# Joining two weight groups at the start, moving constant loads, and forming norm factors in columns

## The chip, the cores and the metric

The kernel runs on one core of one Trainium2 chip. The metric is device time in microseconds (us) of the whole kernel; lower is better. The engines are PE (TensorE, matrix products), DVE (VectorE), ACT (ScalarE), POOL (GpSimd) and SP (SyncE, which here only issues DMAs). Each engine works through its own instructions strictly in the order in which they stand.

## The reference, cut to what matters

Two transformer blocks of width 2048 run one behind the other on 256 tokens, all in float32. Every projection is preceded by a root-mean-square norm:

```python
def rmsnorm(x, g):
    x32 = x.astype(jnp.float32)
    y = x32 * lax.rsqrt(jnp.mean(x32 * x32, axis=-1, keepdims=True) + EPS)
    return (y * g.astype(jnp.float32)).astype(x.dtype)
...
    hn = rmsnorm(h, norm_mix_g)
    proj = hn @ w_in + b_in          # q, k, v, gates, conv inputs
    ... mLSTM, conv, merge: h = h + merged @ w_out
    hn = rmsnorm(h, norm_ffn_g)      # up, depthwise conv, silu, down
    ...
    return rmsnorm(h, norm_out_g)    # and the second block starts:
h = rms_norm(x, g_pre); y = gla_mixer(h, ...); x = x + rms_norm(y, g_post)
h = rms_norm(x, g_pre); y = mla_mixer(h, ...); x = x + rms_norm(y, g_post)
# in mla_mixer: c_q, c_kv, k_rope, gate = split(h @ w_in)
#   q = rms_norm(c_q, g_qa) @ w_qb ; kv = rms_norm(c_kv, g_kva) @ w_kvb
```

The norm factor is one number for each token. The kernel multiplies by it after the projection, so a projection need not wait for it, but its results do.

## The kernel before, in words

All weights are read once, as one stream of pieces of about 1 MB that SP issues in a fixed order into three buffers (`raw`). A piece has two halves of up to 1040 columns, called subs here. For each sub ACT writes the rounded high part and DVE the remainder into a tile `hl` (lines 312 and 313); there are four such tiles, and the split is asked for three subs ahead of use (`LOOK`). Activations are held with features on the 128 partitions and tokens along the row, split in the same way (`xhl`, lines 434 and 435).

PE multiplies group by group. A group of kind A has blocks of 128 output features; each unit (a block of weights for one k of 16) is a pair of matmuls, 512 and 256 columns (lines 359 and 360). A group of kind B (`v`, `gv`) has tokens on the partitions and 344 features along the row, three matmuls for each k and each half of the tokens (lines 372 to 374). Results stand in two double accumulators in PSUM (`acc`) and are taken out by `evac`: ACT copies one half to `t`, DVE adds the other (`u`, lines 412 and 413).

At the start the x tiles `h`, the first weight pieces and then the constants (`con`, with the identity and a matrix of ones; `vec`, with gains and biases) come through SP. The first groups are four `qk` groups (a head's q and k blocks each), then three `v` groups. POOL meanwhile works through some 55 instructions that make the angle tables for the rotary embedding (`rope_tables`), and behind those, in its own order, issues the three DMAs of the `v` bias (`vb`, line 731). The results of the first `v` group (`ifc`, line 735) need `vb`; three matmuls into the second `v` group, PE transposes `ifc` (line 654).

A norm factor is formed in two shapes. `bc_sum` multiplies a matrix of ones by the squares, which puts the sum of every token on all partitions, a row of 256 numbers; ACT takes the root and DVE the reciprocal of 128x256 (`rsqrt`, lines 465 and 466). `col_sum` gives the same sums as two columns of 128 tokens, one token on a partition. The places that matter are `mk_R1` (row `R` and column `Rc` of the first norm, within the fourth `qk` group), `mk_R3` (behind the second block's first q and k groups: output norm of block one and the next norm combined, rows `Ro` and `R`, column `Rc`), the last input norm (`st6`, in the first `mgate` group) and `low_rank_scale` (factors `sq` and `skv`, after the second `mgate` group). In `mk_R3`, `Rc` is needed by `gkc` (line 892), which PE transposes three matmuls into the second `gv` group (line 902). POOL multiplies `h` by `Ro` (`x2_scale`, line 1001).

Instructions come in program order except for a priority: what stands in `tc.high_priority(offset=150)` is ordered as if written 150 places earlier. `tc.issue_after(st["mm"])` puts a small matmul behind the last group's.

Of the kernel before, what the change touches and what calls it, by code (L numbers as in the profile page):

```python
# [8 lines left out]
F32 = mybir.dt.float32  # L9
F32R = mybir.dt.float32r  # L10
I32 = mybir.dt.int32
AF = mybir.ActivationFunctionType
ALU = mybir.AluOpType

P = 128
T = 256
D = 2048
KD = D // P
# [11 lines left out]
VB = 344  # L30
# [4 lines left out]
def _blk(start, n=P):  # L35
    return np.arange(start, start + n)
# [9 lines left out]
def plan():  # L46
# [14 lines left out]
        g.append(dict(name=name, kind=kind, blocks=blocks, k0=k0, nk=nk, n=nk * n, order=order))  # L61

    W = "w_in"
    for h in range(4):
        add("qk", "A", [(W, _blk(h * P)), (W, _blk(512 + h * P))], 0, KD)
    vcols = np.concatenate([_blk(3072, 8), _blk(1024, 1024)])
    for c in range(3):
# [175 lines left out]
def build(tc, a, dump=None):  # L243
# [26 lines left out]
    def vc(name, i):  # L270
        return vec[:, vw[name] + i:vw[name] + i + 1]
# [4 lines left out]
    def tt(name="t"):  # L276
        return tp.tile([P, 2, T], F32, tag="t2", name=name)

    def sm(name="sm"):
        return smp.tile([P, 512], F32, tag="sm", name=name)  # L280
# [15 lines left out]
    def piece_dma(p, x, y_):  # L296
        at, n = pieces[p]
        src = stream[P * at:P * (at + n)].rearrange("(p n) -> p n", p=P)
        nc.sync.dma_start(raws[p][:, x:y_], src[:, x:y_])

    def need(q_):
        while st["sub"] <= min(q_, len(subs) - 1):
            q = st["sub"]
            p, half = divmod(q, 2)
            emit_dma(p + RAW - 1)
            n = subs[q]
            o = subs[q - 1] if half else 0
            hl = hlp.tile([P, 2, SUB], F32R, tag="hl", name="hl")
            cuts = (0, n) if q else (0, n // 2, n)
            for x, y_ in zip(cuts, cuts[1:]):  # L310
                src = raws[p][:, o + x:o + y_]
                S.activation(hl[:, 0, x:y_], src, AF.Copy)  # L312
                V.tensor_tensor(hl[:, 1, x:y_], src, hl[:, 0, x:y_].bitcast(F32), op=ALU.subtract)  # L313
            hls[q] = hl
            if half == 1:
                raws.pop(p, None)
            hls.pop(q - 8, None)
            st["sub"] += 1
# [87 lines left out]
    def bc2(r):  # L406
        return r[:, None, :].to_broadcast([P, 2, T])

    def evac(ps, nb=2):
        t, u = tt("t"), tt("u")  # L410
        with tc.high_priority(offset=150):
            S.activation(halves(t[:, :nb]), out_of(ps[:, :nb, T:2 * T]), AF.Copy)  # L412
            V.tensor_tensor(halves(u[:, :nb]), out_of(ps[:, :nb, 0:T]), halves(t[:, :nb]), op=ALU.add)  # L413
        return u
# [10 lines left out]
    def split(dst, src, scale=None):  # L425

        v = dst.rearrange("p (a s i) -> p s a i", a=2, s=2)
        hi, lo = v[:, 0], v[:, 1]
        src = halves(src)
        if scale is None:  # L430
            i = S.activation(hi, src, AF.Copy)
            j = V.tensor_tensor(lo, src, hi.bitcast(F32), op=ALU.subtract)
        else:
            i = S.activation(hi, src, AF.Identity, scale=scale)
            j = V.scalar_tensor_tensor(lo, src, scale, hi.bitcast(F32), op0=ALU.mult, op1=ALU.subtract)  # L435
        return i.ins, j.ins
# [26 lines left out]
    def rsqrt(out, in_, scale):  # L463

        S.activation(out, in_, AF.Sqrt, bias=epsc[:out.shape[0]], scale=scale)
        V.reciprocal(out, out)

    def bc_sum(ss):
        ps = sm()
        with tc.issue_after(st["mm"]):  # L470
            PE.matmul(ps[:, 0:T], lhsT=ones, rhs=ss, start=True, stop=True)
        return ps[:, 0:T]

    def col_sum(ss):
        ps = sm()
        for t in range(2):
            with tc.issue_after(st["mm"]):
                PE.matmul(ps[:, t:t + 1], lhsT=ss[:, t * P:(t + 1) * P], rhs=ones[:, 0:1], start=True, stop=True)
        return ps[:, 0:2]

    def out_norm(name, IN, g, y):

# [37 lines left out]
    def lazy(X_, f, ahead):  # L520

        done = [0]

        def get(k):
            while done[0] <= min(k + ahead, KD - 1):
                f(done[0])
                done[0] += 1
            return X_(k)

        return get  # L530
# [17 lines left out]
    xload = lambda x, y_: nc.sync.dma_start(h[:, x:y_], a["xT"][:, x:y_])  # L548
    s0, n0, n1 = subs[0], pieces[0][1], pieces[1][1]
    xload(0, 1)  # L550
    piece_dma(0, 0, s0 // 2)
    xload(1, 2)
    xload(2, 4)
    piece_dma(0, s0 // 2, s0)
    xload(4, 6)
    piece_dma(0, s0, n0)
    xload(6, 8)
    xload(8, 10)
    piece_dma(1, 0, subs[2])
    xload(10, 12)  # L560
    xload(12, 14)
    piece_dma(1, subs[2], n1)
    xload(14, 16)
    emit_dma(2)
    nc.sync.dma_start(con, a["con"])
    nc.sync.dma_start(vec[:, 16:nvec], a["vec"][:, 16:nvec])
    _, X = hl_tiles(2, "xhl")
    need(0)
    for k in range(KD):
        split(X(k), h[:, k], vc("g_mix", k))  # L570
        if k in (2, 6, 10):
            need(k // 4 + 1)
    st1 = Stat("a")

    R = row_tile("R")
# [1 line left out]

    def mk_R1():
        ss = st1.fold(V)
        rsqrt(R, bc_sum(ss), 1.0 / D)  # L580
        rsqrt(Rc, col_sum(ss), 1.0 / D)

    COS, SIN = row_tile("COS"), row_tile("SIN")
    turn = inv_two_pi()
# [46 lines left out]
    def qk_out(hd, u):  # L631
        uR = times_R(u, R)
        S.activation(qk[:, hd, 0], uR[:, 0], AF.Identity, bias=vc("bq", hd))
        V.tensor_scalar(qk[:, hd, 1], uR[:, 1], vc("bk", hd), float(P) ** -0.5, op0=ALU.add, op1=ALU.mult)

    held = []
    for hd in range(4):
        u = evac(dense("qk", X))
        held.append(u)
        for k in ((0, 2, 4), (6, 8, 10), (12, 14), ())[hd]:  # L640
            st1.add(h[:, k:k + 2], eng=V)
        if hd == 2:
            mk_R1()
        if hd >= 2:
            while held:
                qk_out(hd + 1 - len(held), held.pop(0))
    ccol = stp.tile([P, 2, 4], F32, tag="ccol", name="ccol")
    rw = lambda i: rows[0:4, i, :]

# [78 lines left out]

    for c in range(3):
        vb = tt("vb").rearrange("p a t -> p (a t)")  # L730
        nc.gpsimd.dma_start(vb[:, 0:VB], a["bv"][c:c + 1, :].to_broadcast([P, VB]))
        ps = dense("v", X)
        ifc = tt("ifc")
        for t in range(2):
            stt = lambda dst, x, y_: V.scalar_tensor_tensor(dst, ps[:, t, x:y_], Rc[:, t:t + 1], vb[:, x:y_],
                                                            op0=ALU.mult, op1=ALU.add)
            if c == 0:
                stt(ifc[:, t, 0:8], 0, 8)
                stt(vm[:, t, 0:VB - 8], 8, VB)
            else:  # L740
                stt(vm[:, t, c * VB - 8:(c + 1) * VB - 8], 0, VB)
        if c == 0:
            side.append(mlstm_rows(ifc))
        pump()
# [120 lines left out]

    def mk_R3():
        s3, s4 = st3.fold(), st4.fold()
        for (ro, r, f) in ((Ro, R, bc_sum), (None, Rc, col_sum)):
            n = T if f is bc_sum else 2
            w = tt("w")  # L870
            ro = ro if ro is not None else w[:, 1, 0:n]
            rsqrt(ro, f(s3), 1.0 / D)
            t = w[:, 0, 0:n]
            V.tensor_tensor(t, f(s4), ro, op=ALU.mult)
            V.tensor_tensor(t, t, ro, op=ALU.mult)
            rsqrt(t, t, 1.0 / D)
            V.tensor_tensor(r, t, ro, op=ALU.mult)

    gb = big(name="gb")
    gbT = gb[:, 0:2048].rearrange("p (b t) -> p b t", b=8)  # L880
# [185 lines left out]
    gates = big(F32, (P, KD, T), name="gates")  # L1066

    def low_rank_in(which, s, q, ps):
        u = evac(ps)
        s.add(u)  # L1070
        for b in range(2):
            i = 2 * q + b
            split(cqkv[:, 4 * which + i], u[:, b], vc(("g_qa", "g_kva")[which], i))

    def low_rank_scale(s, tag):
        ss = s.fold()
        r = row_tile(tag)
        w = tt("w")
        V.tensor_tensor(w[:, 0], R, R, op=ALU.mult)
        V.tensor_tensor(w[:, 1], bc_sum(ss), w[:, 0], op=ALU.mult)  # L1080
        rsqrt(w[:, 1], w[:, 1], 1.0 / 512)
        V.tensor_tensor(r, w[:, 1], R, op=ALU.mult)
        return r

    sa, sb = Stat("a"), Stat(None, gates[:, 14:16])
    ps = dense("cq", X)
# [20 lines left out]
    for j in range(8):  # L1107
        u = evac(dense("mgate", X))
        if j == 0:
            rsqrt(R, bc_sum(st6.fold()), 1.0 / D)  # L1110
            uR = times_R(ukr, R, 1)
            rope([(kr[0:64, 0], 0, 64), (kr[64:128, 1], 64, 128)], uR[:, 0], (V, V, G, G))
        s = times_R(u, R, eng=G)
        S.activation(gates[:, 2 * j:2 * j + 2], s, AF.Silu)
        if j == 1:
            sq_ = low_rank_scale(sa, "sq")
            skv = low_rank_scale(sb, "skv")
        if j == 2:
            pc = sm()
            for t in range(2):  # L1120
                PE.transpose(pc[:, t:t + 1], skv[0:1, t * P:(t + 1) * P], con[0:1, C_ID:C_ID + 1])
            skc = stp.tile([P, 2], F32, tag="Rc", name="skc")
            V.tensor_copy(skc, pc[:, 0:2])

    _, OX = hl_tiles(2, "ohl")
    XQ = lambda k: cqkv[:, k]
# [125 lines left out]
```

## Time and profile before

| | before |
|---|---|
| runs | 2059.97, 2060.18, 2061.51 us; median 2060.18 us |
| profiled execution | 2059.47 us, span 2057.8 us (1.67 us lie around it) |
| PE busy | 2005.0 us, 97% of the span |
| DVE, ACT, POOL busy | 70%, 56%, 19% |
| mean granted clock of TensorE | 0.990 |
| HBM read | 381.52 MB, 186 GB/s over the span |

A PE that is busy 97% of the time sets the time; what can be won is in its idle time, some 53 us, and in stretches in which its clock is granted at half. An engine's idle time elsewhere costs nothing by itself.

### The profile page before, as it was taken

To read this page: it belongs to the slowest core of one execution; us is meant where nothing else is said; L and a number is where in the kernel's file an instruction comes from. 1 tells how busy PE (TensorE), PEld (TensorE's weight loads), DVE (VectorE), ACT (ScalarE), POOL (GpSimd) and SP (SyncE) were. 2 spreads that over 40 slices of the span, in tenths; PEclk is the share of its full clock that TensorE was granted. 3 is DMA by queue.
4 is the path that set the end of the run, shared out by engine and by line. 5 is a ranking of instruction groups with operands and counts; after the bars stand their busy time and mean duration, and the time that the engine had idled before them with its cause. 6 is when DMAs were issued, how large, how long until landed. Compare 5 with 4: busy or idle time off the path is not lost. (4 is left out here: it accounts for less than half of the span.)

```text
span 2057.8 us, 30674 instructions
## 1 busy us (share of the span) xinstructions
PE 2005.0 (97%) x12438; PEld 1849.7 (90%) x12438; DVE 1433.7 (70%) x1758; ACT 1153.3 (56%) x1599; POOL 392.9 (19%) x333
## 2 busy tenths in 40 slices
PE   8799999999999999999999999999999999999997
PEld 7788999999999999999999999989999988989996
DVE  7568776666667888864588876676767558777754
ACT  6454555555556666654466666655666556544453
POOL 8511000010122111100011113321220025112312
PEclk9999999999999999999999999999999999999998
DMA  7443555555555555555555555535545544554343
GB/s 289 155 164 144 204 200 204 191 204 204 205 201 188 205 204 198 198 200 206 203 205 203 197 195 206 205 120 198 180 171 188 201 170 178 194 188 145 109 165 112
DMA packets 55743, 385.61 MB, mean 187 GB/s; under 512 B 6384, under 2 KB 6640, under 8 KB 10544
## 3 DMA queue, kind: packets, MB, share of 16 engines
q1 hardware_dynamic: 55152, 382.91, 51.5%
q8 instruction: 97, 1.59, 0.3%
q0 software_dynamic: 304, 0.73, 0.1%
q14 instruction: 46, 0.38, 0.1%
q10 hardware_dynamic: 144, 0.01, 0.0%
HBM read 381.52 MB, written 2.10 MB: 186 GB/s over the span
## 5 line engine op out<-in xcount | busy, mean ns | idle before, releaser
L313 DVE TENSOR_TENSOR hl<-raw,hl 128x1024 fp32r<-128x1024 f32 (+3 forms) x722 | 941.0, 1311 | 353.3 <-ACT hl L312 352.8
L359 PE MATMUL acc<-xhl,hl 128*128 128x512 f32 x3440 | 1138.1, 384 | 9.5 <-DVE xhl L435 7.8
L312 ACT ACTIVATE hl<-raw 128x1024 fp32r<-128x1024 f32 (+3 forms) x722 | 756.8, 1052 | 395.3 <-PE acc L360 250.5
L360 PE MATMUL acc<-xhl,hl 128*128 128x256 f32 x3440 | 940.9, 274 | 1.6 <-DVE hl L313 1.6
L359 PEld LDWEIGHTS acc<-xhl,hl 128*128 128x128 f32 x3440 | 652.6, 190 | 105.0 <-DVE xhl L435 6.9
L360 PEld LDWEIGHTS acc<-xhl,hl 128*128 128x128 f32 x3440 | 662.7, 193 | 3.3 <-DVE hl L313 2.9
L359 PE MATMUL acc<-ghl,hl 128*128 128x512 f32 x688 | 225.4, 382 | 0.0
L412 ACT ACTIVATE t<-acc 128x512 f32<-128x512 f32 x138 | 82.2, 596 | 192.6 <-PE acc L360 171.8
L360 PE MATMUL acc<-ghl,hl 128*128 128x256 f32 x688 | 187.5, 273 | 0.0
L413 DVE TENSOR_TENSOR u<-acc,t 128x512 f32<-128x512 f32 x138 | 94.9, 688 | 104.3 <-ACT t L412 104.3
L418 POOL TENSOR_TENSOR uR<-u,R 128x512 f32<-128x512 f32 x51 | 69.8, 1369 | 443.3 <-DVE u L413 436.0
L359 PEld LDWEIGHTS acc<-ghl,hl 128*128 128x128 f32 x688 | 130.0, 189 | 18.1
L360 PEld LDWEIGHTS acc<-ghl,hl 128*128 128x128 f32 x688 | 132.1, 192 | 0.0
L456 POOL TENSOR_TENSOR ss<-ss,sq 128x512 f32<-128x512 f32 x41 | 64.9, 1584 | 223.0 <-ACT sq L451 213.6
L374 PE MATMUL acc<-hl,xhl 128*128 128x344 f32 x288 | 90.4, 314 | 1.5 <-DVE hl L313 1.5
L372 PE MATMUL acc<-hl,xhl 128*128 128x344 f32 x288 | 91.0, 316 | 0.0
L373 PE MATMUL acc<-hl,xhl 128*128 128x344 f32 x288 | 90.3, 313 | 0.0
L795 POOL TENSOR_TENSOR m<-u 128x256 f32<-128x256 f32 x16 | 24.9, 1553 | 336.1 <-DVE u L793 336.1
L783 PE MATMUL acc<-hmxc,hl 128*128 128x512 f32 x256 | 84.7, 382 | 0.0
L359 PE MATMUL acc<-mg,hl 128*128 128x512 f32 x256 | 83.9, 382 | 0.0
L831 ACT ACTIVATE cv<-uR,vec 128x256 f32<-128x256 f32 x86 | 46.9, 593 | 57.9 <-POOL uR L418 57.9
L359 PE MATMUL acc<-ohl,hl 128*128 128x512 f32 x224 | 73.7, 383 | 0.0
(515 smaller groups left out, 2490.2 us busy)
## 6 DMA issues: line engine op xcount, KB each, us to landing
raw<-stream SPq DMA_DIRECT2D x330, 1024.0 KB, 4.8
raw<-stream SPq DMA_DIRECT2D x21, 1032.0 KB, 4.8
raw<-stream SPq DMA_DIRECT2D x4, 512.0 KB, 7.2
out<-y SPq DMA_DIRECT2D x8, 256.0 KB, 2.1
h<-xT SPq DMA_DIRECT2D x7, 256.0 KB, 7.2
raw<-stream SPq DMA_DIRECT2D x1, 1028.0 KB, 4.7
raw<-stream SPq DMA_DIRECT2D x1, 1008.0 KB, 4.7
raw<-stream SPq DMA_DIRECT2D x1, 988.0 KB, 6.6
```

What stands on the lines that cost most here:

```text
L312: S.activation(hl[:, 0, x:y_], src, AF.Copy)
L313: V.tensor_tensor(hl[:, 1, x:y_], src, hl[:, 0, x:y_].bitcast(F32), op=ALU.subtract)
L359: PE.matmul(o, lhsT=wh, rhs=both(x), start=(k == 0), stop=False)
L360: mm = PE.matmul(o[:, T:2 * T], lhsT=wl, rhs=part(x, 0), start=False, stop=(k == nk - 1))
L372: PE.matmul(o, lhsT=xh, rhs=both(wh), start=(k == 0), stop=False)
L373: PE.matmul(o, lhsT=xl, rhs=both(wh), start=False, stop=False)
L374: mm = PE.matmul(o, lhsT=xh, rhs=both(wl), start=False, stop=(k == nk - 1))
L412: S.activation(halves(t[:, :nb]), out_of(ps[:, :nb, T:2 * T]), AF.Copy)
L413: V.tensor_tensor(halves(u[:, :nb]), out_of(ps[:, :nb, 0:T]), halves(t[:, :nb]), op=ALU.add)
L418: (eng or V).tensor_tensor(w[:, :nb], u[:, :nb], bc2(R)[:, :nb], op=ALU.mult)
L456: (eng or G).tensor_tensor(self.ss, self.ss, sq, op=ALU.add)
L783: PE.matmul(o, lhsT=wh, rhs=both(x), start=(k == 0), stop=False)
```

## The change

The first two `qk` groups become one group of four blocks, which runs over the first eight k for all four blocks, then over the last eight for two blocks at a time. The x tiles are split as the group asks for them (`lazy`), not all ahead; the first weights come in smaller cuts, later x tiles in larger ones. The two evictions of the joined group, and one pair in the last layer, are taken out of the early order (`ahead=0`). `con` and the rest of `vec` are loaded behind this group. The squares of `h` are added during the third and fourth `qk` groups, and `mk_R1` with all four `qk_out` follows the fourth. `vb` is loaded through SP. At `mk_R1`, `mk_R3`, the last input norm and `low_rank_scale` only the two columns are formed (`second` combines two norms in a column), and `to_row` spreads a column along the row: DVE multiplies the identity by the column (`dg`), PE multiplies ones by `dg`, ACT copies the result.

```diff
-    for h in range(4):
+    add("qk", "A", [(W, _blk(o + h * P)) for h in range(2) for o in (0, 512)], 0, KD)
+    for h in (2, 3):
         add("qk", "A", [(W, _blk(h * P)), (W, _blk(512 + h * P))], 0, KD)
...
-            cuts = (0, n) if q else (0, n // 2, n)
+            cuts = (0, n) if q else (0, n // 4, n // 2, n)
...
-    def evac(ps, nb=2):
+    def evac(ps, nb=2, ahead=150):
         t, u = tt("t"), tt("u")
-        with tc.high_priority(offset=150):
+        with tc.high_priority(offset=ahead):
...
+    def to_row(dst, c_):
+
+        dg, pr = tt("dg"), sm()
+        for t in range(2):
+            V.tensor_scalar(dg[:, 0, t * P:(t + 1) * P], ident, c_[:, t:t + 1], None, op0=ALU.mult)
+            with tc.issue_after(st["mm"]):
+                PE.matmul(pr[:, t * P:(t + 1) * P], lhsT=ones, rhs=dg[:, 0, t * P:(t + 1) * P], start=True, stop=True)
+        S.activation(dst, pr[:, 0:T], AF.Copy)
...
+    def second(dst, c_, total, n):
+
+        w = col_tile("cw")
+        V.tensor_tensor(w, total, c_, op=ALU.mult)
+        V.tensor_tensor(w, w, c_, op=ALU.mult)
+        rsqrt(w, w, 1.0 / n)
+        V.tensor_tensor(dst, w, c_, op=ALU.mult)
...
-    nc.sync.dma_start(con, a["con"])
-    nc.sync.dma_start(vec[:, 16:nvec], a["vec"][:, 16:nvec])
+    xload(12, 16)
     _, X = hl_tiles(2, "xhl")
-    need(0)
-    for k in range(KD):
-        split(X(k), h[:, k], vc("g_mix", k))
-        if k in (2, 6, 10):
-            need(k // 4 + 1)
+    X_ = X
+    X = lazy(X_, lambda k: split(X_(k), h[:, k], vc("g_mix", k)), 4)
...
         ss = st1.fold(V)
-        rsqrt(R, bc_sum(ss), 1.0 / D)
         rsqrt(Rc, col_sum(ss), 1.0 / D)
+        to_row(R, Rc)
...
     held = []
+    ps = dense("qk", X)
+    nc.sync.dma_start(con, a["con"])
+    nc.sync.dma_start(vec[:, 16:nvec], a["vec"][:, 16:nvec])
+    held += [evac(p_, ahead=0) for p_ in ps]
+    X = X_
+    for hd in (2, 3):
+        for k in range(8 * hd - 16, 8 * hd - 8, 2):
+            st1.add(h[:, k:k + 2], eng=V)
+        held.append(evac(dense("qk", X)))
+    mk_R1()
     for hd in range(4):
-        u = evac(dense("qk", X))
-        held.append(u)
...
+        qk_out(hd, held[hd])
...
-        nc.gpsimd.dma_start(vb[:, 0:VB], a["bv"][c:c + 1, :].to_broadcast([P, VB]))
+        nc.sync.dma_start(vb[:, 0:VB], a["bv"][c:c + 1, :].to_broadcast([P, VB]))
...
         s3, s4 = st3.fold(), st4.fold()
-        for (ro, r, f) in ((Ro, R, bc_sum), (None, Rc, col_sum)):
...
+        t3, t4 = col_sum(s3), col_sum(s4)
+        c3 = col_tile("c3")
+        rsqrt(c3, t3, 1.0 / D)
+        second(Rc, c3, t4, D)
+        to_row(R, Rc)
+        to_row(Ro, c3)
...
-    def low_rank_scale(s, tag):
-        ss = s.fold()
+    def low_rank_scale(s, tag, c6):
+        c_ = col_tile("c" + tag)
+        second(c_, c6, col_sum(s.fold()), 512)
         r = row_tile(tag)
...
+        to_row(r, c_)
+        return r, c_
...
-            rsqrt(R, bc_sum(st6.fold()), 1.0 / D)
+            c6 = col_tile("c6")
+            rsqrt(c6, col_sum(st6.fold()), 1.0 / D)
+            to_row(R, c6)
...
-            sq_ = low_rank_scale(sa, "sq")
-            skv = low_rank_scale(sb, "skv")
-        if j == 2:
-            pc = sm()
-            for t in range(2):
-                PE.transpose(pc[:, t:t + 1], skv[0:1, t * P:(t + 1) * P], con[0:1, C_ID:C_ID + 1])
-            skc = stp.tile([P, 2], F32, tag="Rc", name="skc")
-            V.tensor_copy(skc, pc[:, 0:2])
+            sq_, _ = low_rank_scale(sa, "sq", c6)
+            skv, skc = low_rank_scale(sb, "skv", c6)
```

Lines of the changed kernel lie up to 17 higher than those of the kernel before. SP's queue at the start, before (`raw` are weight pieces, `h` x tiles; pieces of 2064 columns belong to the `v` groups):

```order
L299 DMA raw<-stream 128x2048
L565 DMA con<-con 128x1408
L566 DMA vec<-vec 128x564
L299 DMA raw<-stream 128x2048 x5
L299 DMA raw<-stream 128x2064 x8
```

The same queue now:

```order
L569 DMA h<-xT 128x1024
L300 DMA raw<-stream 128x2048 x5
L653 DMA con<-con 128x1408
L654 DMA vec<-vec 128x564
L300 DMA raw<-stream 128x2064 x5
L748 DMA vb<-bv 128x344
L300 DMA raw<-stream 128x2064 x2
L748 DMA vb<-bv 128x344 x2
```

The constants moved behind five more weight pieces, and `vb` now stands on SP, the first behind the fifth `v` piece; the fifth to eighth `v` pieces are used by the second and third `v` groups.

DVE at `mk_R3`, before, from the eviction of the k group (`w` are scratch, `q_` and `uR` use the row `R`, `gkc` and `vg` use the column `Rc`):

```order
L413 TENSOR_TENSOR u<-acc,t 128x512
L466 RECIPROCAL R<-R 128x256
L313 TENSOR_TENSOR hl<-raw,hl 128x1032
L874 TENSOR_TENSOR w<-sm,R 128x256
L466 RECIPROCAL w<-w 128x2
...
L466 RECIPROCAL w<-w 128x256
L466 RECIPROCAL w<-w 128x2
L313 TENSOR_TENSOR hl<-raw,hl 128x1032
L877 TENSOR_TENSOR R_11748<-w,R 128x256
L877 TENSOR_TENSOR Rc<-w 128x2
L1007 SCALAR_TENSOR_TENSOR q__11952<-u,R_11748 128x512
```

DVE at the same place now (`c_11936` is the column `c3`):

```order
L467 RECIPROCAL c_11936<-c_11936 128x2
L497 TENSOR_TENSOR cw<-sm,c_11936 128x2
L498 TENSOR_TENSOR cw<-cw,c_11936 128x2
L314 TENSOR_TENSOR hl<-raw,hl 128x1032
L467 RECIPROCAL cw<-cw 128x2
L314 TENSOR_TENSOR hl<-raw,hl 128x1032
L500 TENSOR_TENSOR Rc<-cw,c_11936 128x2
L486 TENSOR_SCALAR dg<-con,Rc 128x128 x2
L486 TENSOR_SCALAR dg<-con,c_11936 128x128 x2
L314 TENSOR_TENSOR hl<-raw,hl 128x1032
L1020 SCALAR_TENSOR_TENSOR q__11959<-u,R_11752 128x512
```

The operations on 128x256 are gone, `Rc` stands behind two weight splits (`hl`), not four, and four `dg` are new. On PE the four matmuls that read `dg` stand 39 matmuls into the first `gv` group.

ACT at `low_rank_scale`, before, from the eviction of the second `mgate` group (`gates` is a silu of another table):

```order
L412 ACTIVATE t<-acc 128x512
L312 ACTIVATE hl<-raw 128x1024
L1114 ACTIVATE gates<-uR 128x512
L465 ACT_TABLE_LOAD
L465 ACTIVATE w<-w,epsc 128x256 x2
L312 ACTIVATE hl<-raw 128x1024 x3
```

ACT there now:

```order
L413 ACTIVATE t<-acc 128x512
L466 ACT_TABLE_LOAD
L466 ACTIVATE cw<-cw,epsc 128x2
L1126 ACT_TABLE_LOAD
L1126 ACTIVATE gates<-uR 128x512
L489 ACTIVATE sq<-sm 128x256
L466 ACT_TABLE_LOAD
L466 ACTIVATE cw<-cw,epsc 128x2
L313 ACTIVATE hl<-raw 128x1024 x2
L489 ACTIVATE skv<-sm 128x256
```

The two roots, one instruction pair before, are now apart with the silu between them, which takes two more table loads, and the weight splits stand behind both.

## Rows read from the trace of the kernel before

**Rows 1.** The page, part 1: busy us (share of the span) and instructions.

```profile
PE 2005.0 (97%) x12438; PEld 1849.7 (90%) x12438; DVE 1433.7 (70%) x1758; ACT 1153.3 (56%) x1599; POOL 392.9 (19%) x333
```

**Rows 2.** Waits of PE: waiter, waited for: us in total, times, longest.

```profile
PE sm L654 <- DVE ifc L735: 10.6, 1, 10.6
PE acc L359 <- DVE xhl L435: 7.8, 6, 2.6
```

**Rows 3.** Timeline of PE at three waits: start, duration, idle before.

```profile
50.38 0.70 PE L471 MATMUL sm<-ss,con 128*128 128x256 f32 x2 [1.17 <-DVE ss L460]
...
81.60 0.37 PE L654 MATMUL sm<-con,ifc 128*4 128x128 f32 x1 [10.61 <-DVE ifc L735]
...
1355.58 0.38 PE L902 MATMUL sm<-con,gkc 128*16 128x128 f32 x1 [4.67 <-DVE gkc L892]
```

**Rows 4.** Windows: PE, PEld, DVE, ACT, POOL busy; clock; DMA share, GB/s.

```profile
10.00:15.00 5.00, 3.29 (x14) 2.44 (x14) 4.08 (x7) 4.60 (x10) 4.59 (x6) 0.87 1.04 409
...
13.70:17.00 3.30, 3.30 (x13) 2.85 (x12) 3.30 (x6) 3.30 (x7) 3.05 (x3) 0.50 1.05 421
...
82.00:84.00 2.00, 2.00 (x8) 2.00 (x8) 2.00 (x5) 0.00 (x0) 0.00 (x0) 0.50 0.10 23
84.00:86.00 2.00, 2.00 (x11) 1.67 (x11) 0.35 (x2) 1.40 (x2) 0.00 (x0) 0.66 0.00 0
86.00:88.00 2.00, 2.00 (x16) 2.00 (x15) 1.11 (x2) 1.95 (x3) 0.00 (x0) 1.00 0.20 29
...
1358.00:1360.00 2.00, 2.00 (x13) 1.95 (x12) 0.13 (x1) 1.33 (x2) 0.00 (x0) 0.87 0.76 320
```

**Rows 5.** Timeline of DVE and of POOL at the wait of line 654.

```profile
81.32 0.23 DVE L735 SCALAR_TENSOR_TENSOR ifc<-acc,Rc,vb 128x8 f32<-128x8 f32 x1 [11.90 <-DMA vb<-bv]
...
77.99 1.70 POOL L731 DMA_DIRECT2D vb<-bv  x3
```

**Rows 6.** DMA issues: KB each, median us from issue to landing.

```profile
con<-con SPq DMA_DIRECT2D x1, 704.0 KB, 9.5
vb<-bv POOLq DMA_DIRECT2D x3, 172.0 KB, 3.5
```

**Rows 7.** Timeline of DVE in `mk_R3`.

```profile
1343.57 0.14 DVE L874 TENSOR_TENSOR w<-sm,w 128x2 f32<-128x2 f32 x1
1343.75 1.05 DVE L875 TENSOR_TENSOR w<-w 128x2 f32<-128x2 f32 x1
...
1345.87 1.76 DVE L466 RECIPROCAL w<-w 128x256 f32<-128x256 f32 x2
...
1350.75 1.22 DVE L877 TENSOR_TENSOR Rc<-w 128x2 f32<-128x2 f32 x1
```

**Rows 8.** Timeline of ACT at the start and at `mk_R3`.

```profile
10.47 1.06 ACT L312 ACTIVATE hl<-raw 128x1024 fp32r<-128x1024 f32 x1 [0.40 <-DMA raw<-stream]
...
33.31 0.60 ACT L412 ACTIVATE t<-acc 128x512 f32<-128x512 f32 x1 [1.56 <-PE acc L360]
...
43.79 0.60 ACT L412 ACTIVATE t<-acc 128x512 f32<-128x512 f32 x1 [1.56 <-PE acc L360]
...
1334.75 0.60 ACT L412 ACTIVATE t<-acc 128x512 f32<-128x512 f32 x1 [1.55 <-PE acc L360]
1335.37 1.28 ACT L465 ACT_TABLE_LOAD   x1
1336.66 0.47 ACT L465 ACTIVATE R<-sm,epsc 128x256 f32<-128x256 f32 x1
```

**Rows 9.** Timeline of PE in `mk_R3`; a float32 matmul leaves two records.

```profile
1334.55 1.03 PE L471 MATMUL sm<-ss,con 128*128 128x256 f32 x4
1335.42 0.95 PE L478 MATMUL sm<-con,ss 128*128 128x1 f32 x8
1336.23 0.39 PE L372 MATMUL acc<-hl,xhl 128*128 128x344 f32 x1
```

**Rows 10.** Groups by line and shape: busy us, mean ns of one, idle before.

```profile
L516 DVE TENSOR_SCALAR dg<-con,oc 128x128 f32<-128x128 f32 x4 | 1.0, 283 | 0.1
```

More of the change, by code (lines that the diff above doesn't have):

```diff
@@ L479, in col_sum, with col_tile @@
         return ps[:, 0:2]
+    def to_row(dst, c_):
[5 more added lines that the diff above has]
+        S.activation(dst, pr[:, 0:T], AF.Copy)
+    def col_tile(tag):
+        return stp.tile([P, 2], F32, tag=tag, name=tag)
+    def second(dst, c_, total, n):
[4 more added lines that the diff above has]
+        V.tensor_tensor(dst, w, c_, op=ALU.mult)
     def out_norm(name, IN, g, y):
@@ L550, in build @@
     xload(0, 1)
-    piece_dma(0, 0, s0 // 2)
+    piece_dma(0, 0, s0 // 4)
+    piece_dma(0, s0 // 4, s0 // 2)
     xload(1, 2)
+    piece_dma(0, s0 // 2, s0)
     xload(2, 4)
-    piece_dma(0, s0 // 2, s0)
+    piece_dma(0, s0, n0)
     xload(4, 6)
-    piece_dma(0, s0, n0)
+    piece_dma(1, 0, subs[2])
     xload(6, 8)
[L558 to L561, printed above, removed]
     piece_dma(1, subs[2], n1)
-    xload(14, 16)
+    xload(8, 12)
     emit_dma(2)
-    nc.sync.dma_start(con, a["con"])
-    nc.sync.dma_start(vec[:, 16:nvec], a["vec"][:, 16:nvec])
+    xload(12, 16)
     _, X = hl_tiles(2, "xhl")
-    need(0)
-    for k in range(KD):
-        split(X(k), h[:, k], vc("g_mix", k))
-        if k in (2, 6, 10):
-            need(k // 4 + 1)
+    X_ = X
+    X = lazy(X_, lambda k: split(X_(k), h[:, k], vc("g_mix", k)), 4)
     st1 = Stat("a")
@@ L636, in build @@
     held = []
-    for hd in range(4):
-        u = evac(dense("qk", X))
-        held.append(u)
[L640 to L646, printed above, removed]
+    ps = dense("qk", X)
[8 more added lines that the diff above has]
+    mk_R1()
+    for hd in range(4):
+        qk_out(hd, held[hd])
     ccol = stp.tile([P, 2, 4], F32, tag="ccol", name="ccol")
@@ L867, in mk_R3 @@
         s3, s4 = st3.fold(), st4.fold()
-        for (ro, r, f) in ((Ro, R, bc_sum), (None, Rc, col_sum)):
[L869 to L877, printed above, removed]
+        t3, t4 = col_sum(s3), col_sum(s4)
[4 more added lines that the diff above has]
+        to_row(Ro, c3)
     gb = big(name="gb")
@@ L1068, in low_rank_in @@
     def low_rank_in(which, s, q, ps):
-        u = evac(ps)
+        u = evac(ps, ahead=150 if which else 0)
         s.add(u)
@@ L1073, in low_rank_in @@
             split(cqkv[:, 4 * which + i], u[:, b], vc(("g_qa", "g_kva")[which], i))
-    def low_rank_scale(s, tag):
-        ss = s.fold()
+    def low_rank_scale(s, tag, c6):
+        c_ = col_tile("c" + tag)
+        second(c_, c6, col_sum(s.fold()), 512)
         r = row_tile(tag)
[L1078 to L1083, printed above, removed]
+        to_row(r, c_)
+        return r, c_
     sa, sb = Stat("a"), Stat(None, gates[:, 14:16])
```

## The prediction

> **What bounds the kernel now.** I read the page first, to see whose time counts: PE is busy 2005.0 of 2057.8 us [rows 1], so a change can gain only where PE stands idle (52.8 us in all) or runs at half clock. The list of PE's waits comes next, longest first; the reader should see one wait of 10.6 us at line 654, and behind it 7.8 us in six waits on `xhl` [rows 2], which belong to the step into the last layer, are set there by POOL's adds into `h`, and are not touched. Then the timeline at each wait that the change does touch: 1.17 us before the sum of the first norm, 10.61 us before the transposes of `ifc`, 4.67 us before those of `gkc` [rows 3]. Last the windows: after a long wait TensorE's granted clock is at its lower level, and the same matmuls go half as fast. In 82 to 84 us it is 0.50 with 8 records, in 86 to 88 us 1.00 with 16 [rows 4]. Such a stretch costs half its length on top of the wait.
>
> Two lengths recur. Between 1336.23 and 1350.91 us (1355.58 less 4.67) PE runs 99 matmuls of a `v`-like group [rows 3, 9], 0.148 us each. A group of 32 pairs takes 43.79 - 33.31 = 10.48 us [rows 8]: 0.164 us a matmul, 2.62 us a sub. Below, +x is x us after the last matmul of the group named.
>
> **1. `vb` goes through SP.** DVE waited 11.90 us for `vb` alone [rows 5]. POOL issued it at 77.99 us, after all of `rope_tables`, and it landed 3.5 us after issue [rows 5, 6]: the place in POOL's order is the whole delay. Lost are 10.61 us and the cold stretch behind: from 81.60 to 85.36 us (0.66 in the 84-86 window means 1.36 us of it at half), 3.76 us, half of it 1.9 us; I count 1.8. Together 12.4.
>
> What comes late next? The first `vb` stands on SP behind the fifth `v` piece, whose buffer comes free when DVE has split the fourth `v` sub, about +4.4 after the fourth `qk` group, and it waits for PE to have read `dg` of `mk_R1`, about +3.6 (step 3). So issue at about +4.8. With the 3.5 us of its own rows it lands at +8.3, with the 9.5 us of `con`, which came through a full queue [rows 6], at +14.3. It is needed at +15.9, when PE has done the column sums (0.4), a wait of 0.9, the spread (0.44) and 96 matmuls (14.2). Both fit. Queued behind it on SP are the sixth and later `v` pieces; the sixth is not due before the split of the sixth `v` sub, past +11, and its data only at about +28, so the wait on SP hides under the three subs of lead. Residue at the transposes: `ifc` follows the last matmul by one DVE operation, PE has three matmuls (0.44 us) until then; I leave 0.2. **Gain 12.2**, bounds 8 and 12.4.
>
> A rule speaks against this step. The Trainium skill, DMA: Bandwidth & Descriptors, section Issuing engines are not separate DMA queues, says that DMAs of all issuing engines share the same 16 engines, so that another issuer saves only issue time, usually small. By it alone step 1 would gain next to nothing. The rows put the loss ahead of the transfer, in the issue at 77.99 us.
>
> **2. `mk_R3` in columns.** Before, `Rc` stood behind two 128x256 reciprocals and four splits, and POOL's multiplication of `h` by `Ro` ran at the same time: a 128x2 product took 0.14 us without and 1.05 and 1.22 us with such company; the reciprocals take 1.76 each [rows 7]. `Rc` was ready at 1351.97 us, `gkc` later still. Lost: 4.67 us and half of the cold stretch from 1355.58 to 1358.52 (0.87 in the window is 0.52 us at half [rows 4]), 1.5 us; together 6.1.
>
> Now: `t` runs +0.2 to +0.8, the table load to +2.1 [rows 8], the root of two columns ends at +2.35 to +2.6; reciprocal and two products at 0.14 to 0.2 each: +2.9. The second root stands behind a split on ACT (1.06): +3.7. On DVE the reciprocal and `Rc` stand behind one split each, paced by PE's subs: `Rc` at about +6.2 (1340.8 us, 11 us earlier). Four `dg` at 0.28 [rows 10]: +6.5 to +7.3. PE gets there after 0.81 for the sums [rows 9] and 39 matmuls, 5.8: +6.6. Wait 0.3, and 0.2 at the transposes of `gkc`. **Gain 5.6**, bounds 2 (DVE's splits come late and `dg` with them) and 6.1. `Ro` comes some 4 us later; POOL's 15 us behind it then overlap `gkc`'s DVE work less than the old chain, and nobody waits for `h` there.
>
> **3. `mk_R1`.** The wait of 1.17 us for the folded squares goes [rows 3]: the last sum now stands two splits ahead of the group's end. New is PE's wait for `dg`: table load to +2.1, root +2.35, reciprocal, two `dg`: +2.9 and +3.15. PE is there after 0.4 and 12 matmuls (1.8) at +2.2. Waiting 0.9. **Gain 0.3**, bounds -1.4 and 1.2. Behind the waiting matmul stands only the first `v` group. DVE's four `uR` now come in one block until about +9; the splits behind are still ahead of PE by the three-sub lead (7.9 us), which is their cover.
>
> **4. Last input norm and low-rank factors.** No wait before. PE's own work: `bc_sum` costs 0.43 (two in 0.87), `col_sum` 0.40 (two in 0.81) [rows 9]; a spread, two matmuls of 128 columns, I put at the 0.43 of one of 256. At `mk_R1` and `mk_R3` this cancels. Here three sums and two small transposes (1.5) become three column sums and three spreads (2.5): 1.0 more. The waits: the first spread is wanted at +2.2 (0.4 and 11 matmuls) and ready by about +2.3; `sq`'s at +3.2 (17 matmuls) and ready at +3.3; `skv`'s at +7.3 and ready at +7.0, though behind two more table loads (2 x 1.28), a silu and a copy. I take 0.2. From about +1.6 to +7.2 neither ACT nor DVE splits a sub; the fourth sub of the third `mgate` group is then split at about +8.6 and wanted at +9.5. That cover is 0.9 us thin; if it is gone, each us of lateness costs one. **Loss 1.2**, bounds 0.9 and 5.
>
> **5. The joined start.** Two groups ended at about 33.1 us (0.2 before 33.31 [rows 8]) where 64 pairs need 20.96. The second sub came to ACT at 10.47 us after a wait for its DMA [rows 8], behind 1792 KB; now it stands behind 1536, at 409 GB/s [rows 4] 0.64 us earlier. And eight x tiles, not sixteen, are wanted within the first 32 pairs, so DVE is no longer behind PE. But PE still has eight pairs until about 12 us, and a similar idle share came ahead of the 3.3 us at clock 0.50 (13.7 to 17.0 [rows 4]); I let that stretch stand. **Gain 1.1**; it could be 2.7 if the cold stretch (1.65) goes too, or -2 if the later x tiles, in larger loads, hold DVE up. The constants behind five pieces are wanted some 20 us later, and add about 1 MB in a time when the queue moves half its peak: nothing. The eviction order moves one split ahead of an eviction whose accumulator is wanted half a group later: nothing.
>
> **Sum.** 12.2 + 5.6 + 0.3 - 1.2 + 1.1 = 18.0. The profiled execution took 2059.47 us (span 2057.8), 0.7 below the median of the three runs; 2059.5 - 18.0 = **2041.5 us**.
>
> **The rivals.**
> - *A change of table holds ACT longer than its row.* Five loads lie on the way to a spread (one each in steps 2, 3 and `sq`, two for `skv`). If each held ACT as long again, 1.28 us, PE would wait 6.4 us more: 2047.9. Against: `t` ends at 1335.35, the load runs 1335.37 to 1336.65, the root starts at 1336.66 [rows 8]; there is no gap on either side. The Trainium skill, ScalarE: Activation LUTs, section What ACT_TABLE_LOAD costs, gives 1283 ns for the load and about 1380 ns more for a drain at each switch; by that figure, as an estimate, the five would cost 6.9 and the time be 2048.4. This case's rows agree with the first figure and show nothing of the second. Chance 0.10.
> - *`vb` still late.* If only the issuer changes and not the landing, step 1 gives nothing: 2053.7. It begins to cost when `vb` lands past +15.9, which is 11 us after its issue; `con`'s 9.5 us speaks against it. Chance 0.08.
> - *The start gives nothing or costs up to 2 us*, because ACT and DVE split in the new order as late as before: 2042.6 to 2044.6. For it: both were near full from 10 to 15 us (4.60 and 4.08 of 5 [rows 4]). Chance 0.20.
> - *`Rc` stays late in `mk_R3`,* behind the two splits: 3 us given back, 2044.5. Chance 0.12.
> - *The other side:* each of the five spreads becomes a wait like that of line 902, 4.67 us and 1.5 of cold clock, because PE stands in its own order until DVE has built `dg`. 2059.5 - 12.2 - 1.1 - 1.2 - 6.1 + 5 x 6.2 + 1.0 = 2070.9. It turns to no gain where a spread costs 3.9 us on average, to slower at 4.7. Against: PE has 1.8 to 5.8 us of matmuls ahead of each, and the chains are no more than 0.9 longer. Chance 0.03.
>
> **How the numbers follow.** My own sum has 0.47, and a range of its own from 2038 to 2043. With the rivals of the start, of `Rc` and of the table, 0.89 lie between 2036 and 2049; cutting the lower end to 2038 (start and clock at their best together, about 0.05) leaves some 8 in 10 and a little more. A measurement of this kernel tells 0.2% (4.1 us) from no change; all cases but the last are beyond it. Faster 0.95, same 0.03, slower 0.02.
>
> **What would show it.** Right: DVE's wait on `vb` gone, and the 10.61 us at the `ifc` transposes under 0.5 with the clock at 1.00 behind; the wait at `gkc` under 0.5; new waits on `dg` of about 0.9 at `mk_R1` and 0.3 at `mk_R3`, almost none later; the eviction of the fourth `qk` block pair about 1 us earlier than 33.3. Wrong: a wait on the DMA of `vb` or on SP; a gap around ACT's table loads; `dg` waits above 1.5 us or a window at clock 0.50 behind one; splits (`hl`) as what PE waits for in the third `mgate` group.

## The result and the profile after

| | before | changed |
|---|---|---|
| median of 4 runs | 2060.65 us | 2041.22 us (2039.77 to 2042.13) |
| ratio | | 0.9905, 95% interval 0.9888 to 0.9922 |
| span of the profiled execution | 2057.8 us | 2040.0 us |

The first part of the page, of the changed kernel: busy us, share of the span, instructions. PE's own work is almost what it was [rows 1]; what went is idle time.

```profile
PE 2004.2 (98%) x12460; PEld 1849.2 (91%) x12460; DVE 1429.6 (70%) x1764; ACT 1156.7 (57%) x1605; POOL 390.9 (19%) x330
```

PE's waits in the changed kernel (us in total, times, longest). The 10.6 us for `ifc` are gone from the list [rows 2], `gkc` has 1.1 in two waits where it had one of 4.7 [rows 3], and the wait for a spread (`dg`, line 488) is new, with 0.6.

```profile
PE acc L360 <- DVE xhl L436: 6.5, 5, 2.6
...
PE sm L915 <- DVE gkc L905: 1.1, 2, 0.8
...
PE sm L488 <- DVE dg L486: 0.6, 1, 0.6
```

The timeline of PE at the same places: the spread of `mk_R1`, the transposes of `ifc`, those of `gkc`.

```profile
54.54 0.82 PE L488 MATMUL sm<-dg,con 128*128 128x128 f32 x4 [0.58 <-DVE dg L486]
...
67.94 0.27 PE L671 MATMUL sm<-con,ifc 128*4 128x128 f32 x1
...
1335.96 0.28 PE L915 MATMUL sm<-con,gkc 128*16 128x128 f32 x1 [0.31 <-DVE gkc L905]
1338.18 0.28 PE L915 MATMUL sm<-con,gkc 128*16 128x128 f32 x1 [0.78 <-DVE gkc L905]
```

SP's first `vb`, and DVE's operation that needs it. DVE now waits for PE's accumulator, not for a DMA [rows 5].

```profile
56.59 0.42 SPq L748 DMA_DIRECT2D vb<-bv  x1
```

```profile
67.66 0.23 DVE L752 SCALAR_TENSOR_TENSOR ifc<-acc,Rc,vb 128x8 f32<-128x8 f32 x1 [0.75 <-PE acc L375]
```

Windows behind both transposes (PE, PEld, DVE, ACT, POOL busy; granted clock; DMA share, GB/s): the clock stays at 1.00, where it was 0.50 to 0.87 before [rows 4].

```profile
68.00:70.00 2.00, 2.00 (x16) 1.73 (x16) 2.00 (x4) 0.44 (x1) 1.83 (x3) 1.00 0.94 326
...
1336.00:1338.00 2.00, 1.41 (x9) 1.14 (x9) 2.00 (x2) 0.00 (x0) 2.00 (x2) 1.00 0.34 115
```

Laid side by side, the two profiled executions give where the 17.8 us of the span came from, by the start of the same instruction in each: 2.47 us at the end of the first 64 pairs (ACT's `t` at 33.31 before [rows 8], 30.84 now), 0.46 more by the last matmul ahead of the `ifc` transposes, 12.44 at these transposes and the stretch behind them, 4.73 from there to the `gkl` products (PE's next work on the transposed `gkc`, behind the `gv` groups); then 0.93 lost up to the last of PE's waits for `xhl` in the step into the last layer, 1.08 lost in the last input norm and the low-rank factors, and some 0.3 lost behind them.

```profile
30.84 0.60 ACT L413 ACTIVATE t<-acc 128x512 f32<-128x512 f32 x1 [1.56 <-PE acc L361]
```

### The profile page after: what moved, and what is told of

Read it like the earlier page. It is cut to its first block, busy times and chain, and to the rows that moved or that the text cites. A ratio compares the mean times of both kernels' runs of the same rounds, so it can differ in the third digit from the quotient of the medians.

```text
span 2040.0 us, 30725 instructions
## 1 busy us (share of the span) xinstructions
PE 2004.2 (98%) x12460; PEld 1849.2 (91%) x12460; DVE 1429.6 (70%) x1764; ACT 1156.7 (57%) x1605; POOL 390.9 (19%) x330
## 5 line engine op out<-in xcount | busy, mean ns | idle before, releaser
L314 DVE TENSOR_TENSOR hl<-raw,hl 128x1024 fp32r<-128x1024 f32 (+2 forms) x723 | 945.4, 1316 | 349.3 <-ACT hl L313 348.6
L313 ACT ACTIVATE hl<-raw 128x1024 fp32r<-128x1024 f32 (+2 forms) x723 | 757.1, 1050 | 381.7 <-PE acc L361 251.9
```

## The experiments

Medians are of 4 or 5 runs each, beside runs of the kernel before on the same chip (medians 2060.05 to 2060.98).

**`vb` through SP, nothing else.** The kernel before with one line changed:

```diff
-        nc.gpsimd.dma_start(vb[:, 0:VB], a["bv"][c:c + 1, :].to_broadcast([P, VB]))
+        nc.sync.dma_start(vb[:, 0:VB], a["bv"][c:c + 1, :].to_broadcast([P, VB]))
```

> The kernel before with one line changed: vb is loaded by SP, not POOL. Theory (the delay of vb is its place in POOL's order): the 10.61 us wait at the ifc transposes and the 1.8 us at half clock behind it go, so about 12.3 us less than before, 2048; DVE waits for vb under 1 us. Rival 1 (which engine issues a DMA hardly matters): 2058 to 2061, the wait stays above 9 us. Rival 2 (vb gets stuck behind weight pieces on SP): the wait moves to SP's queue, 2050 to 2058.

2048.03 us (2046.75 to 2048.13), ratio 0.9937 (0.9920 to 0.9953): 12.7 less than the 2060.7 beside it. The wait at the transposes is gone: DVE's `ifc` follows PE, with the load issued at 54.59 us. The first theory holds; one line is worth two thirds of the change.

```profile
70.77 0.23 DVE L735 SCALAR_TENSOR_TENSOR ifc<-acc,Rc,vb 128x8 f32<-128x8 f32 x1 [1.17 <-PE acc L374]
```

**`vb` back on POOL in the changed kernel.** The same line the other way.

> The changed kernel with vb back on POOL. Theory (POOL reaches vb's issue at about 78 us by its own angle work, whatever PE does): vb lands at about 81.5 us, PE is at the ifc transposes at 67.9, so it waits 13.6 us and then runs some 1.8 us behind at half clock: 15.4 more than the changed kernel, 2056.6; what the start and mk_R1 won (3.05 us) is then swallowed in that wait. Rival 1 (the gains add up): 12.3 more, 2053.5. Rival 2 (the issuer hardly matters): 2041.

2054.25 us (2052.53 to 2054.51): 13.0 more than the changed kernel, so neither 15.4 nor nothing, and near the sum of the gains. My theory was wrong in one point: POOL's time of arrival isn't fixed. It came to `vb` at 74.64 us, 3.35 earlier than before [rows 5], and PE waited 8.87 us. The profile is of the fastest of the five runs (2052.53); in it the wait and the half clock behind it cost 10.2 us, not 13.0. What the other runs lost beyond that, no trace shows.

```profile
74.64 1.71 POOL L748 DMA_DIRECT2D vb<-bv  x3
```

```profile
78.58 0.37 PE L671 MATMUL sm<-con,ifc 128*4 128x128 f32 x1 [8.87 <-DVE ifc L752]
```

1.8 of the 3.35 us are there from the first step: POOL's first multiplication of the angle work starts at 6.79 us, at 8.55 before, as the load of `pos` ahead of it landed earlier. The rest is in the angle work itself, which took 67.85 us from there to the issue of `vb`, and 69.44 before.

**`vb` on POOL, but ahead of the angle work.** The kernel before, with the first load moved forward on the same engine, into a part of the `v` buffer that is written last:

```diff
+    vb0 = qkv[:, 4096 - VB:4096]
+    nc.gpsimd.dma_start(vb0[:, 0:VB], a["bv"][0:1, :].to_broadcast([P, VB]))
     rope_tables()
```

> The kernel before with the first vb load still issued by POOL, but ahead of the angle work, into a part of the v buffer that is written last; the second and third vb stay on POOL behind the angle work. Theory (the place in the issuing engine's order is the whole delay, not the engine): as with vb on SP, 2048, no wait at the ifc transposes above 0.3 us. Rival 1 (POOL's DMA queue itself is slow): 2055 or more. Rival 2 (the second vb, issued at 78 us, is late for the second v group): 2048 to 2052, a wait of PE behind the second v group at about 85 us.

2050.80 us (2048.80 to 2051.64). PE has no wait at the `ifc` transposes, so the place in the order was the delay, not the engine that issues, and rival 1 falls; nor is there a wait behind the second `v` group. The 2.8 us over the kernel with SP's load arose elsewhere: in the profiles 2.03 of them are there when the second group ends (35.51 and 33.48 us). In that profile PE waited 1.94 us for the high part of the first sub's second half and ran at half clock until about 20 us, where the kernel with SP's load kept 1.00; the load queue moved 253 GB/s from 5 to 10 us, and 307 in the kernel before. That this small early load was the reason was not separated from chance.

```profile
10.00:15.00 5.00, 3.85 (x11) 2.61 (x11) 2.86 (x5) 3.79 (x8) 3.84 (x4) 0.50 1.02 397
15.00:20.00 5.00, 5.00 (x18) 4.27 (x17) 5.00 (x8) 4.23 (x8) 4.59 (x6) 0.52 1.04 420
```

**`mk_R3` as before, in the changed kernel** (rows by `bc_sum`, four operations of 128x256, the column behind them).

> The changed kernel with mk_R3 formed as before (rows by bc_sum and 128x256 reciprocals, the column behind them). Theory: the 4.67 us wait at the gkc transposes and the half clock behind it come back, 4.7 us in all: 2046. Rival (the wait at gkc came from the splits or the DMA at that place and went with the shift of the start): within 1 us of 2041.2, wait at gkc under 2 us.

2047.06 us (2045.01 to 2047.58), 5.8 more. The wait is back to the hundredth, at half clock behind it:

```profile
1340.16 0.38 PE L919 MATMUL sm<-con,gkc 128*16 128x128 f32 x1 [4.68 <-DVE gkc L909]
```

From PE's last sum over `hsq` (squares in the first block's mixer, at 176 us) to the `gkl` products this stage is 5.7 us longer than in the changed kernel. Its profile gains 2.5 us elsewhere, 1.5 of them behind the `mq` wait (see the last section), which is why its span is only 3.3 longer.

**The last norm and the low-rank factors as rows, in the changed kernel.**

> The changed kernel with the last input norm and the low-rank factors formed as rows, as before. Theory (the columns cost 1.0 us of PE work there and next to no wait): 1.0 less, 2040.2; the stretch from the first mgate group to the third is 1.0 shorter. Rival (the columns cost nothing, or the rows make waits of their own now): 2041.2 or more.

2040.53 us (2039.70 to 2042.32): 0.7 less, inside the scatter of the runs. The trace decides: from the last wait for `xhl` to PE's first wait for `mq`, the buffer of the last layer's projections, it takes 132.90 us, as before, and 133.98 in the changed kernel. The columns cost 1.08 us there, as expected.

**The start as before, in the changed kernel** (two groups, tiles split ahead, constants early).

```diff
-    add("qk", "A", [(W, _blk(o + h * P)) for h in range(2) for o in (0, 512)], 0, KD)
-    for h in (2, 3):
+    for h in range(4):
...
-    X = lazy(X_, lambda k: split(X_(k), h[:, k], vc("g_mix", k)), 4)
+    for k in range(KD):
+        split(X(k), h[:, k], vc("g_mix", k))
...
     emit_dma(2)
+    nc.sync.dma_start(con, a["con"])
```

> The changed kernel with the start of the kernel before (two separate first qk groups, all x tiles split ahead, the old order of the loads and of the constants), mk_R1 and everything behind it as changed. Theory (the joined start is worth about 2 us: the second eviction's t starts at 30.8, 30.8, 31.8 and 32.4 us in four profiles with the joined start and at 33.3 and 33.5 in two without): 2.0 more than the changed kernel, 2043.2, and t of the second group at 33.3 to 33.5. Rival 1 (worth the 1.1 of the prediction): 2042.3. Rival 2 (the difference is the granted clock alone, which falls or not from one execution to the next with the same program): no difference, 2041.2.

2044.31 us (2043.83 to 2044.54), 3.1 more, and `t` of the second group at 33.35. The start is worth more than the 1.1 of the prediction, and not by the clock: here it stayed at 1.00 (a matmul of 512 columns took 0.38 us) and the group ended no earlier than in the profile of before, because PE waited for DVE's splits in place of it.

```profile
16.69 0.38 PE L360 MATMUL acc<-xhl,hl 128*128 128x256 f32 x1 [1.13 <-DVE hl L313]
20.17 0.38 PE L360 MATMUL acc<-xhl,hl 128*128 128x256 f32 x1 [0.59 <-DVE hl L313]
```

**All x tiles split ahead, the rest of the start as changed.**

> The changed kernel with all x tiles split ahead of the joined group in program order, not as the group asks for them. Theory (DVE is near full until 20 us, and what helps is that only eight of the sixteen x tiles are split by the time of the first 32 pairs): the second sub's remainder comes later, PE waits 1 to 3 us more before 20 us, 2042.5 to 2044. Rival (the order of the splits doesn't matter, the loads set the pace): 2041.2.

2042.37 us (2041.34 to 2042.91), 1.2 more than the changed kernel, and `t` at 32.32, which lies among the six profiles of the joined start (30.75 to 32.41). Inconclusive: neither theory's number, and too near to the scatter.

**The constants early, the rest of the start as changed.**

```diff
     xload(12, 16)
+    nc.sync.dma_start(con, a["con"])
+    nc.sync.dma_start(vec[:, 16:nvec], a["vec"][:, 16:nvec])
```

> The changed kernel with the two loads of constants (704 and 282 KB) back ahead of the fourth weight piece, behind the last x tiles. Theory (the pieces they push back by some 2.4 us are needed later than that): 2041.2, no wait of PE on a raw piece. Rival (the place of the constants is what the start gained by): 1 to 2.4 more, up to 2043.6, with ACT waiting for the DMA of a raw piece between 15 and 30 us.

2044.52 us (2042.83 to 2046.35), 3.3 more, as much as undoing the whole start: my "nothing" was wrong. `t` of the joined group came at 35.98, later than with two groups. PE has two waits that the changed kernel hasn't, 2.57 us together, and the clock, at 0.74 from 30 to 35 us, added to them.

```profile
27.57 0.48 PE L360 MATMUL acc<-xhl,hl 128*128 128x512 f32 x1 [1.63 <-ACT hl L313]
28.99 0.44 PE L361 MATMUL acc<-xhl,hl 128*128 128x256 f32 x1 [0.94 <-DVE hl L314]
```

The 986 KB had gone through a queue that was full (418 GB/s), at which rate they are 2.4 us. The fourth weight piece landed 11.9 us after its issue at 12.52, at 24.4 us; in the changed kernel 9.0 after 11.83, at 20.9.

```profile
20.00:25.00 5.00, 4.72 (x29) 4.08 (x28) 4.58 (x6) 1.85 (x5) 4.67 (x5) 1.00 1.02 418
```

But the edit changed more than the place of the constants. Here the order of ACT's instructions is another: the eviction `t` stands ahead of the splits of that piece, and ACT idled 4.12 us for PE's accumulator. The piece, landed at 24.4, lay until 26.46. In the changed kernel both splits stand ahead of `t`. So the run shows what this program lost, not how much of it the queue alone would cost.

```profile
25.97 0.60 ACT L413 ACTIVATE t<-acc 128x512 f32<-128x512 f32 x1 [4.12 <-PE acc L361]
26.46 3.89 ACT L313 ACTIVATE hl<-raw 128x1024 fp32r<-128x1024 f32 x4
```

The same place in the changed kernel:

```profile
20.96 2.01 ACT L313 ACTIVATE hl<-raw 128x1024 fp32r<-128x1024 f32 x2 [0.16 <-DMA raw<-stream]
25.51 0.60 ACT L413 ACTIVATE t<-acc 128x512 f32<-128x512 f32 x1 [2.54 <-PE acc L361]
```

**Two groups with the constants late**, run twice, the second time beside the changed kernel itself.

> The changed kernel with two separate first groups, the x tiles split ahead and the old order of the x loads, but with the constants loaded behind the second group, as changed. With this the start is a square: two groups or joined, constants early or late (joined and late 2041.2, joined and early 2044.5, two and early 2044.3). Theory (each start is bound by what is slower, DVE's splits of sixteen x tiles with two groups, the load queue with the joined one, so neither half of the edit gains without the other): 2044.3, t of the second group at 33.3 to 33.5. Rival 1 (the place of the constants is the whole gain): 2041.2, t at 30.8 to 31.8. Rival 2 (each is worth half): 2042.7.

> The same kernel as the one with two first groups and late constants, a second time, since its runs left two readings. By its trace the joined group is worth about 2 us (t of the second group at 33.6 there, at 30.8 to 32.4 in five profiles with the joined group and late constants): then 2.0 above the changed kernel measured beside it, and t again at 33.3 to 33.7. By its median (2041.67) the joined group is worth 0.5 at most and the constants' place 2.6: then within 0.7 of the changed kernel beside it, with t at 32 or less where PE's clock is not halved from 5 to 17 us, as it was in that profile.

> The changed kernel itself, beside the run above. 2041.2; t of the second group's end between 30.8 and 32.4. In the other profiles the granted clock behind the 2.47 us wait ahead of the first mq products (at about 1832 us) was halved in some and not in others, 1.5 us apart; if that is chance, this program's own two profiles and its runs spread by as much, 2039.5 to 2042.5.

2041.67 us (2041.14 to 2043.65) and 2043.47 (2041.37 to 2044.38), with `t` at 33.64 and 33.96; the changed kernel again 2041.14 (2039.08 to 2042.87), `t` at 31.85. All eight runs of each: medians 2042.6 and 2041.1. So the joined group with late constants is worth about 2 us by the traces and 1.4 by the medians; that the place of the constants is the whole gain, as the first run alone read, doesn't hold.

```profile
33.64 0.60 ACT L412 ACTIVATE t<-acc 128x512 f32<-128x512 f32 x1 [1.56 <-PE acc L360]
```

**Both in one:** the rows for the low-rank factors, and DVE's two `gkc` operations next to each other:

```diff
             for t in range(2):
-                V.tensor_scalar(gkc[:, t, 0:16], ps[:, t, 0:16], Rc[:, t:t + 1], None, op0=ALU.mult)
+                with tc.high_priority(offset=40):
+                    V.tensor_scalar(gkc[:, t, 0:16], ps[:, t, 0:16], Rc[:, t:t + 1], None, op0=ALU.mult)
```

> The changed kernel with the last input norm and the low-rank factors as rows, as before (1.0 less of PE's work there), and with the two gkc operations of DVE next to each other, not with a weight split between them (the 0.78 us wait of PE for the second goes). Theory: 1.7 less than the changed kernel, 2039.5, wait at gkc 0.4 instead of 1.1. Rival (either is taken back by a weight split that comes late): 2041.2 or more, with a new wait on hl behind gkc.

2039.46 us (2038.84 to 2040.18), ratio to before 0.9895 (0.9881 to 0.9909). The second wait is gone, and from the `gkc` transposes to the `gkl` products it takes 13.89 us and not 14.83.

```profile
1336.95 0.28 PE L916 MATMUL sm<-con,gkc 128*16 128x128 f32 x1 [0.31 <-DVE gkc L906]
1337.21 0.27 PE L916 MATMUL sm<-con,gkc 128*16 128x128 f32 x1
```

By the traces the two terms are 0.9 and 1.1, together 2.0 us; the medians are 1.8 apart. The intervals of the two ratios overlap, so the medians alone don't show that this version is faster than the changed kernel.

## Why the prediction was right, and where its terms were off

2041.5 was forecast and 2041.22 measured. The steps on `vb` and `mk_R3` carry almost all of the sum, and what they were to remove went. That the two numbers lie within 0.3 us is luck: runs of the changed kernel lie between 2039.1 and 2042.9 us, and in this pair of profiles `mk_R3` came out smaller and the start larger than forecast.

| step | forecast | by the trace |
|---|---|---|
| `vb` through SP | 12.2 | 12.4 |
| `mk_R3` in columns | 5.6 | 4.7 |
| `mk_R1` | 0.3 | 0.5 |
| last norm, low-rank | -1.2 | -1.1 |
| joined start | 1.1 | 2.5 in this profile; 1.8 on average |
| not forecast | 0 | -0.9 by the last `xhl` wait, -0.3 behind `mq` |

The last row is of the size of the scatter. From the `gkl` products to the last `xhl` wait the kernel before took 346.2 us, the changed kernel 347.1 and, in its second profile, 347.8, and the changed kernel with `vb` on POOL, whose work there is the same, 346.2. Behind the fourth `mq` wait the fourteen profiles took 119.3 to 120.1 us.

*`vb`.* Shown from both sides and by the hoist on POOL. The load was issued 56.59 us into the span, 5.0 after the fourth `qk` group's end (4.8 forecast), and the term is right. The rule of the Trainium skill, DMA: Bandwidth & Descriptors, section Issuing engines are not separate DMA queues, that another issuer saves only issue time, usually small, doesn't carry over to this case in its size: the one-line change gave 12.7 us. The part that it explains stands, since POOL with the load ahead of its work did without SP: what counted was what stood ahead of the issue.

*`mk_R3`.* `Rc` was ready 6.2 us after the k group, as forecast, and the spread made PE wait for nothing (0.3 forecast). What failed is the remainder of 0.2 at the `gkc` transposes: it was 1.1, and the sign named for it, a wait under 0.5, didn't come. The first `gkc` follows the accumulator, but the second stood behind a weight split on DVE, which took 2.16 us beside POOL's `h` multiplication, and 1.23 without one. I had written that POOL's work would overlap `gkc`'s less than before; it moved onto it.

```profile
1324.05 1.23 DVE L314 TENSOR_TENSOR hl<-raw,hl 128x1032 fp32r<-128x1032 f32 x1 [0.20 <-ACT hl L313]
...
1327.39 15.20 POOL L1014 TENSOR_TENSOR h<-h,R 128x512 f32<-128x512 f32 x8 [20.03 <-ACT R L489]
...
1335.68 0.22 DVE L905 TENSOR_SCALAR gkc<-acc,Rc 128x16 f32<-128x16 f32 x1
1335.83 2.16 DVE L314 TENSOR_TENSOR hl<-raw,hl 128x1032 fp32r<-128x1032 f32 x1
1337.90 0.22 DVE L905 TENSOR_SCALAR gkc<-acc,Rc 128x16 f32<-128x16 f32 x1
```

The 4.7 of the table is the least that this step was worth. From the last `hsq` sum to the `gkl` products the four profiles with rows took 1179.4 us (the kernel before), 1180.0, 1180.4 and 1180.7; nine with columns took 1174.7 each. That is 4.7 to 6.0 us, 5.5 on average, near the 5.6 forecast, because the half clock behind the same wait of 4.7 us lasted longer in the other three: in the kernel before it was over some 3 us behind the wait [rows 4], and with `vb` on POOL ahead of the angle work, where the wait ended at 1345.39, it lasted until about 1351.

```profile
1348.00:1350.00 2.00, 2.00 (x9) 2.00 (x8) 0.30 (x1) 1.35 (x2) 0.00 (x0) 0.50 0.65 274
1350.00:1352.00 2.00, 2.00 (x12) 2.00 (x12) 0.93 (x1) 0.00 (x0) 0.00 (x0) 0.76 0.27 29
```

*`mk_R1`.* Right in kind; PE waited 0.58 for `dg`, not 0.9.

*Low-rank.* Right. No wait of PE for `dg` there; the cover of the third `mgate` group held.

*The start* is the step that was wrong, in size and in reason. Six profiles with the joined group and late constants end it at 30.75 to 32.41 us, mean 31.6; three with two groups and early constants at 33.31 to 33.48 (a fourth, with the extra load on POOL, at 35.51). So the term is 1.8 on average, not 1.1. In the changed kernel PE waited 1.2 us in all for DVE's remainders up to the end of this group, and 3.3 us with two groups and early constants. "The constants behind five pieces ... nothing" doesn't hold either: in the kernel with the joined group and early constants nothing of the start was won. There a piece landed 3.5 us later, but ACT's changed order delayed its splits too, and the runs don't separate the two. I had priced each edit alone against the pace of the kernel before, in which ACT waited for no piece between 11 and 33 us. Why two groups with late constants ran 1.7 us below those with early ones, though `t` comes no earlier and every stage up to `gkc` is as long, stays open; by the trace it would be nothing, and the scatter of single runs is as large.

*The rivals.* ACT's change of table held it no longer than its row: `t` ended at 1319.99, the load ran to 1321.28, the root began at 1321.30. The same holds where two roots and a silu alternate:

```profile
1751.89 1.28 ACT L466 ACT_TABLE_LOAD   x1
1753.18 0.29 ACT L466 ACTIVATE cw<-cw,epsc 128x2 f32<-128x2 f32 x1
1753.50 1.28 ACT L1126 ACT_TABLE_LOAD   x1
1754.79 0.63 ACT L1126 ACTIVATE gates<-uR 128x512 f32<-128x512 f32 x1
```

Of five spreads one made PE wait, for 0.58 us, so the rival on the other side was far off.

## What to carry to other kernels

A DMA that lands late may be late only because it is issued late: look at what stands ahead of it on the engine that issues it, and move that one line first. When two edits at one place remove two limits that lie close together, price them together; each alone can be worth little. After an edit, compare the order of the instructions on every engine: here a DMA that moved took an eviction ahead of two weight splits on ACT. A short operation on the path should not stand behind a weight split, even of a buffer that has three subs of lead.

## What the runs showed of the hardware

After the same wait, with the same program, PE went on at half clock in some executions and at full clock in others. In the last layer PE waits 2.47 us for DVE to take an accumulator out into `mq`. From this wait to PE's fourth wait for `mq` nine of fourteen profiles took 88.1 to 88.2 us, and five took 86.5. The changed kernel itself did both (windows of the first profile, then of the second):

```profile
1832.00:1834.00 2.00, 2.00 (x5) 1.63 (x6) 2.00 (x4) 0.00 (x0) 0.00 (x0) 0.50 0.76 303
1834.00:1836.00 2.00, 2.00 (x8) 1.61 (x8) 0.65 (x1) 0.00 (x0) 0.00 (x0) 0.74 0.62 221
```

```profile
1834.00:1836.00 2.00, 2.00 (x11) 1.73 (x11) 2.00 (x4) 0.00 (x0) 0.00 (x0) 1.00 0.84 356
```

That is 1.5 us at one place, and the runs of one kernel spread over 0.7 to 3.8 us. The stretch of half clock at the start [rows 4] was of this kind too, which I had taken for part of the kernel: the kernel before with only `vb` on SP kept 1.00 there, and ended its second group at 33.48 us all the same.

The column of the granted clock can miss it. In the first profile of two groups with late constants it says 1.00 from 10 to 15 us, where 13 matmul records fill 4.38 us and a matmul of 512 columns took 0.63 us; in the changed kernel 21 fill 3.84, and such a matmul took 0.38.

```profile
10.00:15.00 5.00, 4.38 (x13) 3.42 (x14) 4.08 (x6) 4.62 (x9) 4.67 (x5) 1.00 1.05 410
```

The same window in the changed kernel:

```profile
10.00:15.00 5.00, 3.84 (x21) 3.09 (x22) 4.74 (x6) 4.31 (x8) 4.75 (x4) 1.00 1.03 419
```
